# Plain fp32 products instead of split ones for the second block's gates and delta net

## The chip, the cores and the metric

One Trainium2 chip, one core. The metric is the device time of one execution, in microseconds (us), as the median of several. The engines are TensorE (PE; its weight loads are shown as PEld), VectorE (DVE), ScalarE (ACT), GpSimd (POOL), and SyncE (SP), which issues most DMAs. The granted TensorE clock is given as a share of full speed.

## The reference

Two blocks of a network on 256 tokens of width 1024, in fp32. The first (two layers of feed-forward, four attentions, feed-forward) isn't touched. The second mixes the tokens with two recurrent branches and then runs a mixture of experts. What matters here is the mixing sublayer, on the normed and modulated input `u_lat`:

```python
split_at = [A_COLS, A_COLS + B_COLS]
a_lat, b_lat, gates_lat = jnp.split(u_lat @ w_in, split_at, axis=-1)
oa_lat, _ = gdn_branch(a_lat, state_a, ...)              # gated delta net, 4 heads of 128
ob_lat, _ = rwkv_branch(to_col_major(b_lat, rows), state_b, ...)   # RWKV-7, 8 heads of 64
g_a, g_b = jnp.split(gates_lat, 2, axis=-1)
y = (sigmoid(g_a) * (o_a @ w_o_a) + sigmoid(g_b) * (o_b @ w_o_b)) @ w_out
```

`w_in` has 2064 columns for the delta net (q, k, v and z of 512 each, 16 for its decay and step), 1920 for the RWKV branch and 2048 for the gates.

## The kernel before, in words

Features lie on the 128 partitions, tokens along the free axis; a 1024-wide input is eight blocks `c` of [128, 256 tokens]. Most matrix products are **split products**: an fp32 operand is written as a high part, rounded by ScalarE (`split`: an activation Copy to fp32r), and a low part, the difference, taken by VectorE; `mm3` (lines 102 to 104) then adds three fp32r matmuls: low weights by high input, high by low, high by high. The weights are split as they arrive: a load `raw` of 1 MB holds 256 columns of all eight blocks, and each 128 columns of it take one ScalarE copy `wh` (L132) and one VectorE difference `wl` (L133), both [128, 1024]. Two raw buffers and three of split parts rotate.

The program is given as code; a scheduler with a model of the engines' times sets the order in which each engine gets its instructions, and each engine then works its queue in order. What is emitted under `high_priority(100000)` goes ahead of other work that is ready. The pools, which decide when a buffer comes free, act on that order too.

The second block's mixing sublayer is `mix` (L2182):

- `begin` norms the input (`norm_pair`, L175) and leaves it as a high part `hh` and a low part `hl`. It also stores both in a DRAM tensor `u_lat`, since SBUF is wanted for other things later. `hr` is the row factor that GpSimd's pow gives.
- `rwkv_proj` projects the RWKV columns (15 groups of 128; split products, evicted from the PSUM tile `pg`).
- `rwkv`, at high priority, treats the heads in two halves, called hf0 and hf1 here. For each: decay factors `first` (products `pw`), `second` (`pm` = A Bt for a chunk, from which DVE cuts `Ur`, `Mr`, `Mak`), the inverse of a unit triangular matrix (`inverse`, L951: diagonal blocks by row steps `Pb`, `Yb` on VectorE, then `ps_inv` matmuls L996 to L1044), the gate `pgate` (L1774, a plain fp32 product), the recurrence over four chunks (`pa` L1630, `psa` L1636, `pSr` L1648, `yr` L1619), and the output `ob`.
- `gdn_z` and `gdn_proj` project the delta net's columns with the same `proj` (L1059): z into `oa`, the 16 columns `ab`, then k, v, q, each through a short convolution `cvo` (L1093).
- `gates_ahead` projects the 2048 gate columns, 256 at a time. A weight load here is 128 KB (one block `c`, 256 columns); the weights are split by ScalarE (L2229) and GpSimd (L2230), and the two parts of the input come back from `u_lat` two blocks at a time (512 KB, two buffers). Tanh goes to a DRAM tensor `ths`.
- `gdn` prepares the delta net's factors, inverts its triangular matrix by the same routine (`U`), and runs its chain over chunks: `pks` (L1302), `pvn`, `pS`, `po`; `gdn_out` norms the result and multiplies it into `oa` (L1760).

Then `merge` (L2251) multiplies `oa` and `ob` by their output weights (split products `pb`), adds them under the gates (`merged`), and `out_proj` multiplies by `w_out` (`acc`). The router and the experts follow; their weights stream at some 350 GB/s with TensorE busy throughout, so this last part moves as a block with the merge's end.

Of the kernel before, what the change touches and what calls it, by code (L numbers as in the profile page):

```python
# [7 lines left out]
F32 = mybir.dt.float32  # L8
F32R = mybir.dt.float32r
I32 = mybir.dt.int32  # L10
AF = mybir.ActivationFunctionType
OP = mybir.AluOpType
# [3 lines left out]
P = 128  # L16
T = 256
D = 1024
KC = D // P
# [12 lines left out]
class Core:  # L32
# [139 lines left out]
        self.nc.vector.tensor_scalar(v, ss[:, 0:1], ss[:, 1:2], eps, op0=OP.add, op1=OP.add)  # L172
        return self.pow(pool, v, "%sr%d" % (name, t))

    def norm_pair(self, pool, x, rs, A, B=None, keep=None, save=None):  # L175

        nc = self.nc
        keep = keep or self.np  # L180
        hh = keep.tile([P, KC, T], F32R, tag="hh", name="hh")
        hl = keep.tile([P, KC, T], F32R, tag="hl", name="hl")
        for t in range(2):
            ts = slice(t * P, t * P + P)
            xn = [pool.tile([P, 512], F32, tag="xn", name="xn", bufs=4) for _ in range(2)]
            xs = [x[:, t, j * 512:j * 512 + 512] for j in range(2)]
            if B is not None:
                for j in range(2):
                    nc.vector.tensor_tensor(xn[j], xs[j], A[:, j], op=OP.mult)
            r = rs(t)  # L190
            for j in range(2):
                js = slice(4 * j, 4 * j + 4)
                if B is None:
                    nc.vector.scalar_tensor_tensor(xn[j], xs[j], r, A[:, j], op0=OP.mult, op1=OP.mult)
                else:
                    nc.vector.scalar_tensor_tensor(xn[j], xn[j], r, B[:, j], op0=OP.mult, op1=OP.add)
                pt = self.ps("s", [P, 4, P], "pt")
                for c in range(4):
                    nc.tensor.transpose(pt[:, c], xn[j][:, c * P:c * P + P], self.ident)
                last = self.split(hh[:, js, ts], hl[:, js, ts], pt)  # L200
            if save is not None:
                for i, v in enumerate((hh, hl)):
                    nc.sync.dma_start(out=save[:, i, :, ts], in_=v[:, :, ts].bitcast(F32))
            if t == 0:
                self.norm_ins0 = last
        self.norm_ins = last + (self.pow_ins,)
        return hh, hl
# [715 lines left out]
class Block2:  # L923
# [135 lines left out]
    def proj(self, u, w, start, n, evict):  # L1059

        k = self.k
        W = k.W
        wide = W.raw // KC
        cs = min(KC, W.part // P)
        for f0 in range(0, n, 256):
            pg = k.ps("g", [P, 2, T], "pg")
            for g0 in range(f0, min(f0 + 256, n), wide):
                m = min(wide, n - g0)
                wr = k.raw(w[:, start + g0: start + g0 + m].rearrange("(c p) f -> p c f", p=P), [P, KC, m])
                for h0 in range(0, m, P):  # L1070
                    mm = min(P, m - h0)
                    fi = (g0 + h0 - f0) // P
                    for c0 in range(0, KC, cs):
                        ws = k.split_w(wr[:, c0:c0 + cs, h0:h0 + mm])
                        for c in range(c0, c0 + cs):
                            k.mm3(pg[:mm, fi], (ws[0][:, c - c0], ws[1][:, c - c0]), (u[0][:, c], u[1][:, c]),
                                  c == 0, c == KC - 1)
            evict(f0 // P, (min(256, n - f0) + P - 1) // P, pg)
# [591 lines left out]
class Tail(Rwkv):  # L1670
# [476 lines left out]
    def begin(self, x, pool):  # L2147


        k, nc, a, R = self.k, self.k.nc, self.a, self.R  # L2150
        self.x1 = self.dram.tile([P, 2, D], F32, name="x1")
        self.u_lat = self.dram.tile([P, 2, KC, T], F32, name="u_lat")
        half = lambda v, q: v[:, q * 512:q * 512 + 512]
        with k.pool("lx", "right") as xp:
            fg, am, bm = [self.gk.tile([P, 2, 512], F32, name=n, tag=tag)
                          for n, tag in (("fg", "cv512"), ("am", "cv1024"), ("bm", "cv0"))]
            nc.sync.dma_start(out=fg.rearrange("p a b -> p (a b)"), in_=bcast_ap(a["final_norm"], D))
            self.row(0, am)
            self.row(1, bm)
            nc.vector.tensor_tensor(am, am, fg, op=OP.mult)  # L2160
            self.hr = self.cst.tile([P, 2], F32, name="hr")

            def both(t):

                xs, xf = [half(x[:, t], q) for q in range(2)], []
                for q in range(2):
                    xf.append(xp.tile([P, 512], F32, tag="mdg", name="xf", bufs=2))
                    nc.vector.tensor_tensor(xf[q], xs[q], fg[:, q], op=OP.mult)
                ss = k.sumsq(xp, xs, "hss")
                v = xp.tile([P, 1], F32, name="hv%d" % t)  # L2170
                nc.vector.tensor_scalar(v, ss[:, 0:1], ss[:, 1:2], 1e-6, op0=OP.add, op1=OP.add)
                ss = k.sumsq(xp, xf, "hsf")
                nc.vector.tensor_tensor(ss[:, 0:1], ss[:, 0:1], ss[:, 1:2], op=OP.add)
                nc.vector.scalar_tensor_tensor(ss[:, 0:1], v, 1e-6, ss[:, 0:1], op0=OP.mult, op1=OP.add)
                r = k.pow(xp, ss[:, 0:1], "hr%d" % t)
                nc.gpsimd.tensor_tensor(self.hr[:, t:t + 1], v, k.mhalf, op=OP.pow)
                return r
            nc.sync.dma_start(out=self.x1, in_=x)
            with k.use(s=k.banks["a"]):
                return k.norm_pair(xp, x, both, am, bm, pool, self.u_lat)  # L2180

    def mix(self, start):  # L2182


        k, a = self.k, self.a
        w = a["w_in_2"][0]
        with ExitStack() as right, ExitStack() as left:
            gk = self.gk = right.enter_context(k.pool("gk", "right"))
            gf = right.enter_context(k.pool("gf", "right"))
            proj = ExitStack()  # L2190
            up = proj.enter_context(k.pool("up", "right"))
            wp = Weights(proj.enter_context(k.pool("uw", "right")), 2048, 2, 1024, 3)
            u = start(up)
            lu = self.lat.enter_context(k.pool("lu"))
            oa = lu.tile([P, 4, T], F32, name="oa")
            ob = lu.tile([P, 4, T], F32, name="ob")
            k.regroup()
            G = dict(a=("a", 3), g=("a", 3), s=("a", 3), w=("w", 1))
            rk = left.enter_context(k.pool("rk"))
            rp = left.enter_context(k.pool("rp"))  # L2200
            with k.use(W=wp):
                self.keep, self.pool, self.t2 = rk, rp, 4
                cols = self.rwkv_proj(u, w, True)
                with k.tc.high_priority(100000):
                    self.rwkv(cols, self.Sb, True, "rl", None, ob)
                with k.use(**G), k.pool("gp", "right") as self.pool:
                    self.keep, self.t2 = gk, 2
                    self.gdn_z(u, w, oa)
                    gcols = self.gdn_proj(u, w, True)
            proj.close()  # L2210
            with k.pool("gm", "right") as self.pool, k.use(W=Weights(gf, 256, 4, 256, 2), **G):
                self.t2 = 4
                self.gates_ahead(gf, a["w_in_2"][0][:, 3984:6032])
                self.gdn_out(self.gdn(gcols, self.Sa, True, "gl"), oa)
        return oa, ob

    def gates_ahead(self, pool, w):

        k, nc = self.k, self.k.nc
        self.ths = self.dram.tile([P, 2 * KC, T], F32, name="ths")  # L2220
        for d in range(0, 2 * KC, 2):
            pg = k.ps("w", [P, 2, T], "pg")
            for c in range(KC):
                if c % 2 == 0:
                    u = pool.tile([P, 2, 2, T], F32, tag="u", name="u", bufs=2)
                    nc.sync.dma_start(out=u, in_=self.u_lat[:, :, c:c + 2])
                wr = k.raw(w[c * P:c * P + P, d * P:(d + 2) * P], [P, 256])
                ws = [k.W.parts.tile([P, 256], F32R, tag=tg, name=tg, bufs=k.W.npart) for tg in ("wh", "wl")]
                nc.scalar.activation(ws[0], wr, AF.Copy)  # L2229
                nc.gpsimd.tensor_tensor(ws[1], wr, ws[0].bitcast(F32), op=OP.subtract)  # L2230
                for j in range(2):
                    js = slice(j * P, j * P + P)
                    k.mm3(pg[:, j], (ws[0][:, js], ws[1][:, js]), (u[:, 0, c % 2].bitcast(F32R), u[:, 1, c % 2].bitcast(F32R)),
                          c == 0 and j == 0, c == KC - 1 and j == 1)
            th = self.pool.tile([P, 2, T], F32, tag="gth", name="gth")
            nc.scalar.activation(th, pg, AF.Tanh, scale=0.5)
            nc.sync.dma_start(out=self.ths[:, d:d + 2], in_=th)
# [193 lines left out]
```

## Time and profile before

| | |
|---|---|
| median of 3 runs | 2395.19 us (2394.86 to 2396.8) |
| profiled execution | 2390.7 us, of which the span 2389.0 |
| mean granted TensorE clock | 0.953 |
| PE busy | 2249.9 us (94%), 19065 records |
| DVE busy | 1689.7 us (71%) |
| ACT busy | 1199.8 us (50%) |
| POOL busy | 344.1 us (14%) |
| first block and the start of the second | 0 to 1616 us |
| second block's mixing sublayer | 1616 to 2032 us |
| out-projection, router, experts | 2032 to 2389 us |

How to read it: a share of the span is a mean over stages that have different limits, so the shares above say little on a change in one stage; the busy times by stage below do. Times in a timeline are from the span's start. A matmul's duration in the trace is longer than its share of the pipeline: one that follows another at once is best priced by the distance between the two starts. A plain fp32 matmul shows up as two records, a split product as three. A row's bracket gives the idle time of the engine before it and what ended it.

### The profile page before, as it was taken

To read this page: it belongs to the slowest core of one execution; us is meant where nothing else is said; L and a number is where in the kernel's file an instruction comes from. 1 tells how busy PE (TensorE), PEld (TensorE's weight loads), DVE (VectorE), ACT (ScalarE), POOL (GpSimd) and SP (SyncE) were. 2 spreads that over 40 slices of the span, in tenths; PEclk is the share of its full clock that TensorE was granted. 3 is DMA by queue.
4 is the path that set the end of the run, shared out by engine and by line. 5 is a ranking of instruction groups with operands and counts; after the bars stand their busy time and mean duration, and the time that the engine had idled before them with its cause. 6 is when DMAs were issued, how large, how long until landed. Compare 5 with 4: busy or idle time off the path is not lost. (4 is left out here: it accounts for less than half of the span.)

```text
span 2389.0 us, 46279 instructions
## 1 busy us (share of the span) xinstructions
PE 2249.9 (94%) x19065; PEld 2041.7 (85%) x19065; DVE 1689.7 (71%) x2796; ACT 1199.8 (50%) x1919; POOL 344.1 (14%) x465
## 2 busy tenths in 40 slices
PE   7999999999999999999999999998989887899997
PEld 6999988897889888888888979998877777799996
DVE  6775575766665674675856668886885866789997
ACT  5554455555443543544554554443553313477775
POOL 2000112121200100100122210002245511000000
PEclk9999999999999989999999999998988668899999
DMA  9676344455434334342545468986445415699992
GB/s 327 223 248 202 111 150 143 140 166 188 142 125 163 132 112 152 128 142 68 173 130 166 143 211 299 331 285 185 125 133 161 146 40 193 239 374 351 353 352 98
DMA packets 325166, 450.91 MB, mean 189 GB/s; under 512 B 16122, under 2 KB 253236, under 8 KB 324564
## 3 DMA queue, kind: packets, MB, share of 16 engines
q1 hardware_dynamic: 324276, 447.06, 55.9%
q8 instruction: 152, 2.49, 0.4%
q0 software_dynamic: 672, 0.82, 0.3%
q14 instruction: 66, 0.54, 0.1%
HBM read 438.09 MB, written 9.76 MB: 187 GB/s over the span
## 5 line engine op out<-in xcount | busy, mean ns | idle before, releaser
L133 DVE TENSOR_TENSOR wl<-raw,wh 128x1024 fp32r<-128x1024 f32 (+1 forms) x703 | 860.0, 1230 | 364.4 <-ACT wh L132 355.2
L132 ACT ACTIVATE wh<-raw 128x1024 fp32r<-128x1024 f32 (+1 forms) x703 | 730.5, 1043 | 465.8 <-PE pg L104 189.5
L102 PE MATMUL pg<-hh,wl 128*128 128x256 f32 x2176 | 627.9, 289 | 4.9 <-DVE wl L133 4.4
L103 PE MATMUL pg<-hl,wh 128*128 128x256 f32 x2176 | 625.9, 288 | 0.4 <-DVE hl L133 0.4
L104 PE MATMUL pg<-hh,wh 128*128 128x256 f32 x2176 | 625.8, 288 | 0.0
L102 PEld LDWEIGHTS pg<-hh,wl 128*128 128x128 f32 x2176 | 420.1, 193 | 17.2 <-issue 6.0
L103 PEld LDWEIGHTS pg<-hl,wh 128*128 128x128 f32 x2176 | 420.0, 193 | 11.1 <-issue 6.6
L104 PEld LDWEIGHTS pg<-hh,wh 128*128 128x128 f32 x2176 | 420.1, 193 | 7.8 <-issue 6.4
L102 PE MATMUL ph<-wh,m0t 128*128 128x256 f32 x512 | 146.4, 286 | 0.0
L102 PE MATMUL acc<-wh,ul 128*128 128x512 f32 x352 | 137.9, 401 | 8.7 <-DVE ul L133 7.0
L103 PE MATMUL ph<-wl,m0t 128*128 128x256 f32 x512 | 144.2, 282 | 0.1
L104 PE MATMUL ph<-wh,m0t 128*128 128x256 f32 x512 | 143.7, 281 | 0.0
L104 PE MATMUL acc<-wh,uh 128*128 128x512 f32 x352 | 140.7, 400 | 0.0
L103 PE MATMUL acc<-wl,uh 128*128 128x512 f32 x352 | 140.4, 399 | 0.0
L103 PE MATMUL acc<-wl,hh 128*128 128x512 f32 (+2 forms) x320 | 120.5, 377 | 0.0
L104 PE MATMUL acc<-wh,hh 128*128 128x512 f32 (+2 forms) x320 | 120.4, 378 | 0.0
L102 PE MATMUL acc<-wh,hl 128*128 128x512 f32 (+2 forms) x320 | 116.9, 381 | 0.5 <-DVE hl L133 0.5
L103 PEld LDWEIGHTS ph<-wl,m0t 128*128 128x128 f32 x512 | 96.5, 189 | 1.2 <-DVE wl L133 0.4
L104 PEld LDWEIGHTS ph<-wh,m0t 128*128 128x128 f32 x512 | 96.5, 188 | 0.5
L102 PEld LDWEIGHTS ph<-wh,m0t 128*128 128x128 f32 x512 | 96.7, 189 | 0.1
L454 ACT ACTIVATE sg<-pg 128x256 f32<-128x256 f32 x80 | 30.8, 385 | 127.4 <-PE pg L104 123.8
L1705 DVE SCALAR_TENSOR_TENSOR adacc<-raw,silu_c,adacc 128x512 f32<-128x512 f32 x112 | 83.4, 747 | 15.3 <-DMA raw<-in_ada_w_dram 14.7
(712 smaller groups left out, 4214.5 us busy)
## 6 DMA issues: line engine op xcount, KB each, us to landing
raw<-in_ffn_w_gu_dram SPq DMA_DIRECT2D x88, 1024.0 KB
raw<-in_w_in_dram SPq DMA_DIRECT2D x56, 1024.0 KB
raw<-in_ffn_w_down_dram SPq DMA_DIRECT2D x44, 1024.0 KB
raw<-in_w_gate_dram SPq DMA_DIRECT2D x32, 1024.0 KB
raw<-in_moe_w_gate_dram SPq DMA_DIRECT2D x32, 1024.0 KB
raw<-in_moe_w_up_dram SPq DMA_DIRECT2D x32, 1024.0 KB
raw<-in_moe_w_down_dram SPq DMA_DIRECT2D x32, 1024.0 KB
raw<-in_ada_w_dram SPq DMA_DIRECT2D x48, 512.0 KB
```

The source lines that it names most:

```text
L102: t.matmul(out, lhs[1], rhs[0], start=start, stop=False)
L103: t.matmul(out, lhs[0], rhs[1], start=False, stop=False)
L104: return t.matmul(out, lhs[0], rhs[0], start=False, stop=stop)
L132: return (nc.scalar.activation(h, src, AF.Copy), nc.vector.tensor_tensor(l, src, h.bitcast(F32), op=OP.subtract))
L133: nc.vector.tensor_tensor(l, src, h.bitcast(F32), op=OP.subtract))
L454: nc.scalar.activation(sg, pg[:, 0], AF.Silu)
L1705: nc.vector.scalar_tensor_tensor(acc, wv, sc, acc, op0=OP.mult, op1=OP.add)
```

## The change

For the second block's tokens, the delta net's projections and the gates use plain fp32 matmuls, with the weights as they are loaded and the input `uf` in full precision. `uf` [128, 8, 256] is a new SBUF tile, written by four GpSimd additions of `hh` and `hl` in `norm_pair`. The store of `u_lat` and its reloads are gone, and the gates' loads are 256 KB each (two blocks `c`), in four buffers. In `proj` the new path reads the raw buffer from TensorE itself. RWKV's projections, the merge and the experts keep split products.

```diff
@@ norm_pair
-            if save is not None:
-                for i, v in enumerate((hh, hl)):
-                    nc.sync.dma_start(out=save[:, i, :, ts], in_=v[:, :, ts].bitcast(F32))
+                if full is not None:
+                    nc.gpsimd.tensor_tensor(full[:, js, ts], hh[:, js, ts].bitcast(F32), hl[:, js, ts].bitcast(F32), op=OP.add)
@@ proj
+                    if not isinstance(u, (tuple, list)):
+                        for c in range(KC):
+                            k.nc.tensor.matmul(pg[:mm, fi], wr[:, c, h0:h0 + mm], u[:, c], start=c == 0, stop=c == KC - 1)
+                        continue
                     for c0 in range(0, KC, cs):
                         ws = k.split_w(wr[:, c0:c0 + cs, h0:h0 + mm])
@@ mix
+            self.uf = gf.tile([P, KC, T], F32, name="uf")
...
-                    self.gdn_z(u, w, oa)
-                    gcols = self.gdn_proj(u, w, True)
+                    self.gdn_z(self.uf, w, oa)
+                    gcols = self.gdn_proj(self.uf, w, True)
...
-            with k.pool("gm", "right") as self.pool, k.use(W=Weights(gf, 256, 4, 256, 2), **G):
+            with k.pool("gm", "right") as self.pool, k.use(W=Weights(gf, 512, 4, 0, 0), **G):
@@ gates_ahead
                 if c % 2 == 0:
-                    u = pool.tile([P, 2, 2, T], F32, tag="u", name="u", bufs=2)
-                    nc.sync.dma_start(out=u, in_=self.u_lat[:, :, c:c + 2])
-                wr = k.raw(w[c * P:c * P + P, d * P:(d + 2) * P], [P, 256])
-                ws = [k.W.parts.tile([P, 256], F32R, tag=tg, name=tg, bufs=k.W.npart) for tg in ("wh", "wl")]
-                nc.scalar.activation(ws[0], wr, AF.Copy)
-                nc.gpsimd.tensor_tensor(ws[1], wr, ws[0].bitcast(F32), op=OP.subtract)
+                    wr = k.raw(w[c * P:(c + 2) * P, d * P:(d + 2) * P].rearrange("(c p) f -> p c f", p=P), [P, 2, 256])
                 for j in range(2):
-                    js = slice(j * P, j * P + P)
-                    k.mm3(pg[:, j], (ws[0][:, js], ws[1][:, js]), (u[:, 0, c % 2].bitcast(F32R), u[:, 1, c % 2].bitcast(F32R)),
-                          c == 0 and j == 0, c == KC - 1 and j == 1)
+                    nc.tensor.matmul(pg[:, j], wr[:, c % 2, j * P:j * P + P], self.uf[:, c],
+                                     start=c == 0 and j == 0, stop=c == KC - 1 and j == 1)
```

The scheduler orders the changed program anew. Three places, with the line numbers of each program (those of the changed one are higher by 3 in this part, lower by 1 within the inverse):

TensorE's queue in hf0's recurrence, before: between `pa` and `psa` of the first chunk stand the transposes `ptk` for the delta net and four gate triples, of which one is shown.

```order
L1630 MATMUL pa<-Sb,AR 64x64 x8
L1105 MATMUL ptk<-ident,l2b 128x128
L1105 MATMUL ptk<-ident,cvo 128x128 x4
L102 MATMUL pg<-u,wl 128x256
L103 MATMUL pg<-u,wh 128x256
L104 MATMUL pg<-u,wh 128x256
...
L1105 MATMUL ptk<-ident,cvo 128x128 x4
L1636 MATMUL psa<-rhs,Ur 64x64 x8
```

The same place after (`pa` is L1633, `psa` L1639, the gate product L2230).

```order
L1622 MATMUL yr<-Sb,AR 64x64 x4
L2230 MATMUL pg<-uf,raw 128x256 x6
L1187 MATMUL rowp<-ident,Be 4x128
L1622 MATMUL yr<-Sb,AR 64x64 x4
L1633 MATMUL pa<-Sb,AR 64x64 x8
L2230 MATMUL pg<-uf,raw 128x256 x11
L1639 MATMUL psa<-rhs,Ur 64x64 x8
L2230 MATMUL pg<-uf,raw 128x256 x5
```

Eleven gate products stand where four triples stood, and the delta net's transposes come later in the queue; in this manner 86 of the 128 gate products lie in hf0's recurrence.

VectorE's queue at the row steps of the second half's inverse (`Pb_19364`, `Yb_19361`), before: they stand alone but for steps of other kinds; those of the delta net's inverse came earlier.

```order
L975 TENSOR_TENSOR Pb_19364<-Ub_19358,Yb_19361 128x49
L977 TENSOR_REDUCE Yb_19361<-Pb_19364 128x7
L975 TENSOR_TENSOR Pb_19364<-Ub_19358,Yb_19361 128x64
L977 TENSOR_REDUCE Yb_19361<-Pb_19364 128x8
L975 TENSOR_TENSOR Pb_19364<-Ub_19358,Yb_19361 128x81
L977 TENSOR_REDUCE Yb_19361<-Pb_19364 128x9
```

After: the steps of the delta net's inverse (`Pb_20715`, `Yb_20712`) and of the second half's alternate.

```order
L976 TENSOR_REDUCE Yb_20712<-Pb_20715 128x11
L974 TENSOR_TENSOR Pb_19364<-Ub_19358,Yb_19361 128x121
L974 TENSOR_TENSOR Pb_20715<-Ub_20709,Yb_20712 128x144
L976 TENSOR_REDUCE Yb_19361<-Pb_19364 128x11
L976 TENSOR_REDUCE Yb_20712<-Pb_20715 128x12
L974 TENSOR_TENSOR Pb_19364<-Ub_19358,Yb_19361 128x144
```

The two inverses that stood one behind the other now run side by side.

TensorE's queue where the delta net's chain begins, before: `pks` stands ahead of the second half's `pgate`, and its chain lies between the steps of that half's recurrence.

```order
L1302 MATMUL pks<-Sak,cvo 128x128 x4
L996 MATMUL ps_inv<-Yc,Q 32x32 x32
L1774 MATMUL pgate<-g_19680,lo 128x256 x2
L1778 MATMUL pv<-ident,vT 128x128 x4
L1619 MATMUL yr<-Sb,AR 64x64 x4
L1308 MATMUL pvn<-r,U 128x128 x4
L1619 MATMUL yr<-Sb,AR 64x64 x4
L1630 MATMUL pa<-Sb,AR 64x64 x8
L1314 MATMUL pS<-bv,kd 128x128 x4
```

After: the last steps of the delta net's inverse (L1036, L1043) lie in the last chunk of that recurrence, and `pks` (L1305) follows.

```order
L1633 MATMUL pa<-Sr,AR 64x64 x8
L1622 MATMUL yr<-Sr,AR 64x64 x8
L1036 MATMUL ps_inv<-D,U 64x64 x8
L1043 MATMUL ps_inv<-U,Q 64x64 x2
L1639 MATMUL psa<-rhs,Ur 64x64 x8
L1043 MATMUL ps_inv<-U,Q 64x64 x11
L1622 MATMUL yr<-SV,Mr 64x64 x8
L1043 MATMUL ps_inv<-U,Q 64x64 x3
L1305 MATMUL pks<-Sak,cvo 128x128 x4
L1311 MATMUL pvn<-r,U 128x128 x4
```

The chain of the delta net so stands behind the recurrence of the second half and not within it.

## Rows read from the trace of the kernel before

**Rows 1.** Busy us (records) by stage: PE, PEld, DVE, ACT, POOL; clock; DMA share; GB/s.

```profile
1633.00:1752.00 119.00, 115.58 (x932) 108.26 (x932) 90.54 (x159) 61.01 (x104) 34.19 (x38) 0.98 0.45 136
1752.00:1776.00 24.00, 16.95 (x120) 14.84 (x121) 22.86 (x63) 10.81 (x25) 8.73 (x13) 0.82 0.55 167
1776.00:1806.00 30.00, 23.32 (x607) 21.04 (x603) 13.44 (x30) 11.69 (x37) 15.31 (x20) 0.69 0.51 143
1806.00:1858.00 52.00, 49.18 (x576) 42.08 (x577) 32.34 (x75) 20.52 (x63) 29.49 (x33) 1.00 0.62 188
1858.00:1886.00 28.00, 20.80 (x121) 17.90 (x119) 23.55 (x53) 8.01 (x21) 13.35 (x19) 0.71 0.46 135
1886.00:1919.00 33.00, 30.95 (x304) 26.54 (x304) 27.55 (x54) 12.68 (x31) 17.11 (x22) 0.68 0.40 116
1919.00:1957.00 38.00, 28.05 (x1008) 26.21 (x998) 23.54 (x63) 5.92 (x12) 4.44 (x9) 0.53 0.16 49
1957.00:1995.00 38.00, 35.05 (x481) 30.68 (x476) 22.79 (x53) 8.31 (x28) 1.67 (x1) 0.90 0.30 101
```

**Rows 2.** Timeline, PE, full clock: start us, us, engine, line, tile, shape, records.

```profile
1214.54 0.59 PE L804 MATMUL sbs<-sbw,m_lt 128*128 128x256 f32 x2
1214.97 0.38 PE L805 MATMUL sbs<-sbw,ones 128*128 128x128 f32 x2
...
1808.07 0.28 PE L103 MATMUL pg<-u,wh 128*128 128x256 f32 x1
1808.19 0.29 PE L104 MATMUL pg<-u,wh 128*128 128x256 f32 x1
```

**Rows 3.** Timeline, PE, at the half clock.

```profile
1957.57 2.08 PE L1774 MATMUL pgate<-g,lo 128*128 128x256 f32 x4
...
1998.70 0.41 PE L102 MATMUL pb<-o,wl 128*128 128x256 f32 x1
1998.91 0.41 PE L103 MATMUL pb<-o,wh 128*128 128x256 f32 x1
```

**Rows 4.** Timeline, POOL, DVE and PE: the waits that the change touches; idle in brackets.

```profile
1628.33 1.40 POOL L2230 TENSOR_TENSOR wl<-raw,wh 128x256 fp32r<-128x256 f32 x2
...
1630.27 1.41 DVE L196 SCALAR_TENSOR_TENSOR xn<-xn,hr,bm 128x512 f32<-128x512 f32 x2 [2.07 <-POOL hr L165]
...
1646.30 0.36 PE L102 MATMUL pg<-u,wl 128*128 128x256 f32 x1 [1.99 <-DMA u<-u_lat]
```

**Rows 5.** Timeline: the first RWKV half's landmarks, PE.

```profile
1750.70 1.16 PE L1563 MATMUL pm<-AR,BK 64*128 64x128 f32 x16
...
1805.90 1.13 PE L1774 MATMUL pgate<-g,lo 128*128 128x256 f32 x4
...
1847.40 0.97 PE L1619 MATMUL yr<-SV,Mr 128*64 128x64 f32 x16
```

**Rows 6.** Costliest lines, 1500 to 2050: count, busy us, mean ns, idle and releasers.

```profile
L133 DVE TENSOR_TENSOR wl<-raw,wh 128x1024 fp32r<-128x1024 f32 (+1 forms) x85 | 106.9, 1262 | 33.0 <-ACT wh L132 32.9
...
L2230 POOL TENSOR_TENSOR wl<-raw,wh 128x256 fp32r<-128x256 f32 x64 | 50.0, 785 | 61.6 <-ACT wh L2229 59.3 <-issue 2.1
```

**Rows 7.** Tile pg alone by stage, columns as in rows 1: after 1806 only gates.

```profile
1806.00:1848.40 42.40, 17.00 (x114) 14.48 (x114) 0.00 (x0) 1.20 (x2) 1.00 0.61 184
1848.40:1886.00 37.60, 15.20 (x78) 12.37 (x78) 0.00 (x0) 1.19 (x2) 0.78 0.52 154
1886.00:1919.00 33.00, 16.08 (x72) 13.87 (x72) 0.00 (x0) 0.96 (x2) 0.68 0.40 116
```

**Rows 8.** Timeline: the end of the inverse, oa, and the merge.

```profile
1938.50 1.02 DVE L985 STREAM_TRANSPOSE Yc<-Ye 128x512 f32<-128x512 f32 x1
...
1994.34 0.75 DVE L1760 SCALAR_TENSOR_TENSOR oa<-pt,rowcols,oa 128x512 f32<-128x512 f32 x1 [0.72 <-PE pt L1758]
...
2013.65 0.55 PE L102 MATMUL pb<-o,wl 128*128 128x256 f32 x1 [3.82 <-DVE merged L251]
...
2031.98 1.08 PE L102 MATMUL acc<-wh,u 128*128 128x512 f32 x4
```

More of the change, by code (lines that the diff above doesn't have):

```diff
@@ L173, in rms, with norm_pair @@
         return self.pow(pool, v, "%sr%d" % (name, t))
-    def norm_pair(self, pool, x, rs, A, B=None, keep=None, save=None):
+    def norm_pair(self, pool, x, rs, A, B=None, keep=None, full=None):
         nc = self.nc
@@ L2151, in begin @@
         self.x1 = self.dram.tile([P, 2, D], F32, name="x1")
-        self.u_lat = self.dram.tile([P, 2, KC, T], F32, name="u_lat")
         half = lambda v, q: v[:, q * 512:q * 512 + 512]
@@ L2179, in begin @@
             with k.use(s=k.banks["a"]):
-                return k.norm_pair(xp, x, both, am, bm, pool, self.u_lat)
+                return k.norm_pair(xp, x, both, am, bm, pool, self.uf)
     def mix(self, start):
@@ L2207, in mix, with gates_ahead @@
                     self.keep, self.t2 = gk, 2
-                    self.gdn_z(u, w, oa)
-                    gcols = self.gdn_proj(u, w, True)
+                    self.gdn_z(self.uf, w, oa)
+                    gcols = self.gdn_proj(self.uf, w, True)
             proj.close()
-            with k.pool("gm", "right") as self.pool, k.use(W=Weights(gf, 256, 4, 256, 2), **G):
+            with k.pool("gm", "right") as self.pool, k.use(W=Weights(gf, 512, 4, 0, 0), **G):
                 self.t2 = 4
-                self.gates_ahead(gf, a["w_in_2"][0][:, 3984:6032])
+                self.gates_ahead(a["w_in_2"][0][:, 3984:6032])
                 self.gdn_out(self.gdn(gcols, self.Sa, True, "gl"), oa)
         return oa, ob
-    def gates_ahead(self, pool, w):
+    def gates_ahead(self, w):
         k, nc = self.k, self.k.nc
```

## The prediction

> **What bounds the kernel now.** I read the busy time by stage first, then the rows around each hand-over. The part that changes is the second block's mixing sublayer, 1633 to 1995 us; what follows it (merge, router, experts) is unchanged and moves with its end. In [rows 1] the reader is to see four kinds of stage. From 1633 to 1752 TensorE is busy 115.6 of 119 us at a granted clock of 0.98: the projections, bound by TensorE. From 1752 to 1806 and again from 1858 to 1957 TensorE has gaps and a clock of 0.53 to 0.82, while VectorE is busy 23.55 of 28, 27.55 of 33 and 23.54 of 38 us: here the small steps of the two triangular inverses and of second() set the pace. From 1806 to 1858 TensorE is busy 49.18 of 52 at full clock: the first RWKV half's recurrence, its pauses filled with gate products. From 1957 to 1995 it is busy 35.05 of 38 with the second half's recurrence and the delta net's chain lying into each other. So more TensorE work costs at once in the first and third kind of stage, and is partly free in the second, where before has put its gate triples; a step less on VectorE pays there.
>
> **The price of one product.** A split product is three records; they start 0.12 us apart, so it costs 0.36 us [rows 2]. Before has plain fp32 products of the same shape (128x128 by 128x256) in another stage: each is two records in the trace, and behind the one at 1214.54 the next line starts 0.43 us later [rows 2]. I take 0.43: +0.07 us each. At the half clock a split record takes 0.21 us, 0.64 for three, and a plain product between 0.85 (twice 0.43) and 1.04 (half of the 2.08 us at 1957.57) [rows 3]. The change has 136 such products in the delta net's projections (eight of them 16 columns wide) and 128 in the gates: 264 x 0.07 = 18.5 us more TensorE work at full clock.
>
> The Trainium skill, "FP8 and Floating Point Precision", section "TensorE Precision Notes", speaks against the change: a true fp32 product makes four passes through the array. If each pass cost the 0.12 us of a split record, the price would be 0.48, the addition 264 x 0.12 = 32 us, and hf0's recurrence below another 4 us longer; the row's 0.43, more than three passes and less than that, decides.
>
> **Ahead of and in the projections.** Two gate splits on GpSimd stand ahead of the norm's pow (1.40 us), and VectorE idles 2.07 us for that pow; one wait of 1.99 us for the reloaded input u stands in the triples [rows 4]. Both go: -3.3 us (1.3 + 2.0). The four gather-adds that write uf lie on GpSimd, which is free there; 38 unsplit triples (14 us) are ahead of uf's first reader. 136 x 0.07 = +9.5; nine gate products come in front of the last projection product (+3.9), four gate triples that before had there are gone (-1.4). The projections' end so comes 8.7 us later on TensorE. But that end isn't what hf0 waits for.
>
> **The first half (hf0), until its recurrence.** Its inverse waits for the last pm (1750.70 in before [rows 5]), and for VectorE, which stands in weight splits then. In after's order all triples come first, so pm's inputs are projected earlier, and the plain products stand behind: I lay the last pm at about 1745. Sixteen wide splits of 1.26 us [rows 6], 20 us of VectorE, are gone from the same stretch, so the inverse's steps find it free. Against it: 15 gate products now lie inside the inverse's matmuls (6.5 us at full clock, 13 at half), where before had gate triples too. Bounds for pgate: 14 us earlier (7 from pm, 7 from VectorE's queue) to 2 later (the projections' 8.7 delay all, less the 7 of VectorE). I take 8 earlier: 1798 instead of 1805.9 [rows 5].
>
> **hf0's recurrence.** In before it lasts from 1805.90 to 1848.37 [rows 5], with 114 gate records in it [rows 7], 38 triples or 13.7 us. After's order puts 86 plain gate products there, five to eleven at each pause, and moves the delta net's pk and pkq out: 86 x 0.43 = 37 us, and the other instructions of that stretch at the durations of the same lines are 17. TensorE was busy 49.18 of 52 us there with less, so nothing hides it: 54 us, last yr at 1852, 4 later than before. No gate product is left then, where before had 150 more records (78 and 72, [rows 7]), 50 triples or 18 us at full clock.
>
> **The tail until the second half's recurrence.** From 1858 to 1957 VectorE is busy 74.6 of 99 us [rows 1]. The two inverses, one mostly behind the other in before, now alternate on VectorE step by step, so each covers the other's waits. The rows of VectorE until both inverses are expanded sum to 73 us by their durations. GpSimd's 64 gate splits of 785 ns (50.0 us) [rows 6] are gone too; what their company costs VectorE no row here prices, so it goes into the lower bound. I take VectorE 90% busy: 73 / 0.9 = 81 us, so 1933 against 1938.5 + 1.0 [rows 8]; bounds 68 (no gap, and 7% off the durations for the company) and 91 (before's own pace, TensorE now at the half clock for want of gates). Before takes 19 us from there to pgate [rows 3, 8], so 1951: 7 us earlier.
>
> **The second half's recurrence and the delta net's chain.** Before runs them together: 1957.57 to oa's end at 1995.1, 37.5 us [rows 3, 8]. After's PE queue has pks of the delta net behind the second half's last psa and yr, since the delta net's inverse is now finished behind the other. The queue is in order, so the chain stands alone: the recurrence without gates 42.5 - 13.7 = 28 us, as in hf0, and then pks to oa, between 20 (half of the shared 37.5) and 38 (all of it); I take 30. 1951 + 58 = 2009, 14 later than before. Bounds of the pair: 48 and 75 (both at the half clock of the stage before).
>
> **Merge.** ob is ready before oa now, so its branch doesn't wait: before's second branch sat 3.82 us for merged [rows 8], and its last product stands ahead of 2031.98, 37 us after oa's end. In after 192 records follow oa without a pause, 0.12 each at full clock (23 us), 0.21 at half (41), with 1.4 us of split ahead; I take 28 + 1.4. End at 2039, 7 us after before's 2032.0 [rows 8].
>
> What costs nothing: the weights' buffers are held longer (16 products of 0.43, 6.9 us for 1 MB, two buffers), that is 152 GB/s, and [rows 1] shows 136 to 188 moved while nothing was short; the gate loads need 256 KB in 1.7 us, also 150. If this cover is gone, each megabyte costs about 2 us more, 17 of them.
>
> **Sum.** -8 (hf0's inverse), +12 (its recurrence: 54 for 42), -10 (from there to the second pgate: 99 for 109), +20 (the pair behind each other: 58 for 37.5), -7 (merge: 30 for 37) = +7 us. The profiled execution took 2390.7 us (span 2389.0), so 2398; the median of the runs shown is 4.5 us above it, so 2402.
>
> **Rivals.** (a) Faster: the relief of VectorE wins. Place: VectorE from 1745 to 1950; price: 20 us of splits, the gate splits' company, and the alternation, which hides the latency of two inverses; it decides once the tail takes less than 74 us, because pgate then stands before 1944 and the 48 us bound of the pair is near, as TensorE's work in it is only 35 us. 1942 + 49 + 29 = 2020, 12 us earlier: 2383. For it: the low busy shares of 1919 to 1957 in [rows 1], which are latency that alternation covers. Against it: hf0's recurrence is TensorE-bound and grows by 12. (b) No change: the pair takes 50 instead of 58, because the delta net's last inverse steps lie inside the recurrence and its pks comes at once: 2394. For it: before itself shows the two threads fit into 37.5 us. Against it: the order of the PE queue. (c) Much slower: without gate products the whole tail is at 0.5 clock, as 1919 to 1957 (0.53) was already in before; then the tail takes its bound of 91 us, pgate stands at 1961, the pair takes 62 (half way between its bounds) and the merge 33: 24 us later than before, 2419. (d) The weights' buffers starve the projections: 17 x 2 = 34 us, 2436.
>
> **Numbers.** Forecast (around 2402, its own range 2398 to 2410) 0.34; (a) 0.30; (b) 0.22; (c) 0.12; (d) 0.02. 0.2% (4.8 us) is about what a measurement of this kernel can tell from no change, so faster is below 2390.4: 0.30; same 0.22; slower 0.48. The range for 8 in 10 leaves out half of (a)'s far end, (d) and part of (c): 2381 to 2422.
>
> **What would show it.** Right: plain products 0.43 us apart; hf0's pgate before 1802; its recurrence 50 us or more with TensorE at 95%; the last gate before 1855; the TensorE clock of the stretch after it near 0.5; pks behind the last psa; pb without a break. Wrong: a plain product at 0.36 or less, or 0.48 and more; pks well before the recurrence's end, or the pair under 50 us (then a or b); gaps of TensorE in the projections that end on a raw load (then d).

## The result, and the profile after

The changed kernel took 2412.8 us (median of 5 runs, 2406.74 to 2416.11) against 2395.95 us (2394.86 to 2398.72) for the kernel before on the same chip: a ratio of 1.0066, 95% interval 1.0051 to 1.0081, 16.9 us slower. The profiled execution took 2409.9 us (span 2408.2), 19.2 us more than that of before. The forecast had 2402, slower, with a range from 2381 to 2422. Single executions of one kernel differ by several us: the profiled execution of before lies 5.3 us under the median here, that of the changed kernel 2.9, so stages are compared below to a few us and kernels by their medians.

Busy times by stage of the changed kernel, the windows of [rows 1] with one more for the merge; columns as there.

```profile
1633.00:1752.00 119.00, 118.78 (x794) 104.68 (x793) 74.96 (x149) 43.77 (x83) 32.63 (x43) 0.99 0.38 116
1752.00:1776.00 24.00, 16.71 (x84) 13.85 (x83) 21.74 (x65) 8.39 (x18) 0.31 (x1) 0.86 0.11 33
1776.00:1806.00 30.00, 26.68 (x627) 22.03 (x626) 7.14 (x14) 4.92 (x8) 2.34 (x4) 0.83 0.36 93
1806.00:1858.00 52.00, 51.65 (x481) 43.38 (x479) 12.02 (x31) 10.98 (x50) 5.88 (x5) 1.00 0.40 114
1858.00:1886.00 28.00, 22.73 (x104) 16.04 (x104) 20.08 (x53) 8.28 (x23) 15.28 (x14) 0.63 0.00 1
1886.00:1919.00 33.00, 25.25 (x169) 18.97 (x169) 29.76 (x63) 8.48 (x20) 14.27 (x18) 0.74 0.00 1
1919.00:1957.00 38.00, 11.88 (x655) 10.76 (x656) 24.33 (x85) 2.21 (x5) 2.32 (x4) 0.50 0.12 35
1957.00:1995.00 38.00, 30.97 (x830) 27.45 (x819) 20.39 (x44) 7.58 (x16) 4.81 (x9) 0.92 0.04 8
1995.00:2060.00 65.00, 54.33 (x365) 49.86 (x366) 46.77 (x63) 23.92 (x44) 9.44 (x5) 0.89 0.70 239
```

The reader is to see three things. From 1806 to 1858 TensorE is busy 51.65 of 52 us with VectorE down from 32.34 to 12.02: TensorE binds it and gate products fill it. From 1858 to 1995 GB/s is 1 to 35, so no gate weight is loaded any more, and from 1919 to 1957 TensorE works 11.88 us where it worked 28.05. And the delta net's chain runs on past 1995, where `oa` was done in before.

The timeline of TensorE in the changed kernel, at the places of [rows 2, 3, 5 and 8]:

```profile
1799.22 1.13 PE L1777 MATMUL pgate<-g,lo 128*128 128x256 f32 x4
...
1845.87 4.91 PE L2230 MATMUL pg<-uf,raw 128*128 128x256 f32 x22
1850.71 0.51 PE L1633 MATMUL pa<-Sr,AR 64*64 64x64 f32 x10
...
1856.83 0.46 PE L1622 MATMUL yr<-SV,Mr 128*64 128x64 f32 x8
...
1960.47 2.07 PE L1777 MATMUL pgate<-g,lo 128*128 128x256 f32 x4
...
1983.93 0.63 PE L1639 MATMUL psa<-rhs,Ur 64*64 64x64 f32 x13
...
1987.04 1.16 PE L1305 MATMUL pks<-Sak,cvo 128*128 128x128 f32 x8
...
2048.22 1.10 PE L102 MATMUL acc<-wh,u 128*128 128x512 f32 x4
```

Eleven gate products (22 records) start at 1845.87 and `pa` follows at 1850.71: 0.44 us for one. The last `psa` of the second half starts at 1983.93 and `pks`, the start of the delta net's chain, behind it, at 1987.04.

With the ends of the operations (`oa` ends at 2019.67) these landmarks cut the sublayer into stages; the same for each kernel that was run, all from one profiled execution each, in us (hf0's recurrence from the first `pgate` to the end of the last `yr`; the last column counts records in the trace, of which some are missing):

| kernel | first pgate at | hf0's recurrence | tail, to second pgate | pair, to oa's end | merge, to first acc | from there to the end | span | gate products behind hf0's recurrence |
|---|---|---|---|---|---|---|---|---|
| before | 1805.9 | 42.5 | 109.2 | 37.5 | 36.9 | 357.0 | 2389.0 | 50 triples |
| changed | 1799.2 | 58.1 | 103.2 | 59.2 | 28.5 | 360.0 | 2408.2 | 0 |
| e1 delta net first | 1796.7 | 58.4 | 97.3 | 40.6 | 28.6 | 362.0 | 2383.6 | 32 |
| e2 before, delta net first | 1813.7 | 44.2 | 97.6 | 41.8 | 35.7 | 359.6 | 2392.6 | 63 triples |
| e3 gates only | 1799.7 | 54.9 | 101.5 | 43.4 | 28.6 | 359.9 | 2388.0 | 0 |
| e4 half the gates | 1801.3 | 39.0 | 105.2 | 54.5 | 27.5 | 359.8 | 2387.3 | 0 |
| e5 e1, chain late | 1801.1 | 58.2 | 97.1 | 53.3 | 27.2 | 358.4 | 2395.2 | 32 |
| e6 e1, 64 held | 1805.1 | 42.1 | 109.1 | 36.2 | 37.5 | 358.2 | 2388.1 | 63 |
| e7 e1, 96 held | 1803.5 | 35.8 | 114.1 | 34.6 | 37.6 | 359.2 | 2384.9 | 88 |
| e8 changed, 64 held | 1799.0 | 35.9 | 112.1 | 63.8 | 27.9 | 359.8 | 2398.5 | 53 |
| e9 e7, gates only | 1798.7 | 40.8 | 107.1 | 45.2 | 32.7 | 362.7 | 2387.1 | 94 |
| e10 e1, 112 held | 1793.8 | 44.0 | 119.0 | 43.9 | 26.9 | 361.0 | 2388.6 | 104 |

From before to the changed kernel: -6.7 (first pgate), +15.6 (recurrence), -6.0 (tail), +21.7 (pair), -8.4 (merge), +3.0 (rest) = +19.2 us.

Not all of this is the change's. The second block's first instruction on VectorE starts 1.8 us earlier in the changed kernel, before anything that was changed; before's line first:

```profile
1616.57 1.28 DVE L189 TENSOR_TENSOR xn<-x,am 128x512 f32<-128x512 f32 x2
```

```profile
1614.79 1.28 DVE L189 TENSOR_TENSOR xn<-x,am 128x512 f32<-128x512 f32 x2
```

Over the twelve kernels it starts between 1614.0 (e1) and 1620.9 (e7), although the first block is the same in all. From this line on, the first `pgate` comes 4.9 us earlier than in before (184.4 for 189.3), not 6.7.

### The profile page after: what moved, and what is told of

The parts are those of the page before. It is cut to its first block, busy times and chain, and to the rows that moved or that the text cites. A ratio compares the mean times of both kernels' runs of the same rounds, so it can differ in the third digit from the quotient of the medians.

```text
span 2408.2 us, 45333 instructions
## 1 busy us (share of the span) xinstructions
PE 2254.1 (94%) x18801; PEld 2025.8 (84%) x18801; DVE 1654.9 (69%) x2779; ACT 1159.7 (48%) x1838; POOL 299.1 (12%) x405
## 5 line engine op out<-in xcount | busy, mean ns | idle before, releaser
L133 DVE TENSOR_TENSOR wl<-raw,wh 128x1024 fp32r<-128x1024 f32 (+1 forms) x686 | 839.8, 1232 | 354.0 <-ACT wh L132 344.0
L132 ACT ACTIVATE wh<-raw 128x1024 fp32r<-128x1024 f32 (+1 forms) x686 | 713.1, 1044 | 452.6 <-PE pg L104 176.9
L102 PE MATMUL pg<-hh,wl 128*128 128x256 f32 x2040 | 587.3, 288 | 3.6 <-DVE wl L133 3.1
L103 PE MATMUL pg<-hl,wh 128*128 128x256 f32 x2040 | 585.5, 287 | 1.6 <-DVE hl L133 1.6
L104 PE MATMUL pg<-hh,wh 128*128 128x256 f32 x2040 | 585.6, 287 | 0.0
L102 PEld LDWEIGHTS pg<-hh,wl 128*128 128x128 f32 x2040 | 393.4, 193 | 14.5 <-issue 5.0
L103 PEld LDWEIGHTS pg<-hl,wh 128*128 128x128 f32 x2040 | 393.3, 193 | 11.4 <-issue 5.9
L104 PEld LDWEIGHTS pg<-hh,wh 128*128 128x128 f32 x2040 | 393.5, 193 | 7.2 <-issue 6.1
L1708 DVE SCALAR_TENSOR_TENSOR adacc<-raw,silu_c,adacc 128x512 f32<-128x512 f32 x112 | 83.7, 749 | 15.7 <-DMA raw<-in_ada_w_dram 14.9
```

The source lines that it names most:

```text
L102: t.matmul(out, lhs[1], rhs[0], start=start, stop=False)
L103: t.matmul(out, lhs[0], rhs[1], start=False, stop=False)
L104: return t.matmul(out, lhs[0], rhs[0], start=False, stop=stop)
L132: return (nc.scalar.activation(h, src, AF.Copy), nc.vector.tensor_tensor(l, src, h.bitcast(F32), op=OP.subtract))
L133: nc.vector.tensor_tensor(l, src, h.bitcast(F32), op=OP.subtract))
L1708: nc.vector.scalar_tensor_tensor(acc, wv, sc, acc, op0=OP.mult, op1=OP.add)
```

## The experiments

Three theories were on record. A: the order does it; gate products, now ready at once, fill the first half's recurrence and push the delta net's preparation back, and its chain then stands alone. B: the price; 264 products cost more on TensorE. C: the clock; without gate products the tail runs at the half clock.

### e1 and e2: the delta net ahead of the gates

The scheduler takes what was emitted first among the work that is ready. e1 is the changed kernel with two lines swapped, e2 the kernel before with the same swap.

```diff
-                self.gates_ahead(a["w_in_2"][0][:, 3984:6032])
                 self.gdn_out(self.gdn(gcols, self.Sa, True, "gl"), oa)
+                self.gates_ahead(a["w_in_2"][0][:, 3984:6032])
```

> The changed kernel with the delta net's scan emitted ahead of the gates, so that a ready gate product no longer goes before the delta net's preparation. Theory A (order: gate products delay the delta net's factors, and its chain then stands alone behind the second half's recurrence): the pair from the second pgate to oa falls from 59 to 38 to 44 us, the first half's recurrence stays within 5 us of its 58, the end comes 12 to 20 us earlier, 2393 to 2401. Theory B (price: 264 products at 0.44 instead of 0.36 are simply more TensorE work): the same work in another order, 2408 to 2414. Theory C (clock: without gate products the stretch from 1858 to 1960 runs at half clock): this order leaves some 40 gate products behind the first half's recurrence, so the clock there rises and a third of the loss comes back, 2405 to 2408.

Measured: 2390.64 us against 2397.79 for before on that chip, ratio 0.9970 (0.9955 to 0.9985). The changed kernel was 0.7% slower than before and is now 0.3% faster with the same work in another order: the order is worth 1% of the time, and A's mechanism holds. It is worth more than A had, as the median lies 2 us under A's range. The pair falls to 40.6 us, as A said; the recurrence stays at 58.4, with 60 gate products in it where the changed kernel has 86, since products for the delta net's factors came in (422 other records for 370). TensorE of e1 from the second `pgate`, and `oa` on VectorE:

```profile
1952.43 2.08 PE L1777 MATMUL pgate<-g,lo 128*128 128x256 f32 x4
...
1957.21 1.16 PE L1305 MATMUL pks<-Sak,cvo 128*128 128x128 f32 x8
1958.61 0.77 PE L1639 MATMUL psa<-rhs,Ur 64*64 64x64 f32 x16 [0.24 <-DVE rhs L1635]
...
1984.08 0.68 PE L1639 MATMUL psa<-rhs,Ur 64*64 64x64 f32 x16
...
1991.59 1.41 DVE L1763 SCALAR_TENSOR_TENSOR oa<-pt,rowcols,oa 128x512 f32<-128x512 f32 x2 [0.19 <-PE pt L1761]
```

`pks` now stands ahead of the first `psa` and not behind the last.

> The kernel before with the delta net's scan emitted ahead of the gates. It tells whether this order is worth the same without the change. Theory A: before already has the delta net's factors in the first half's recurrence and its chain within the second half's, so there is little to win: 2391 to 2399. If the order alone is worth what e1 gains, this run is 12 us or more faster than before, and e1 says nothing on the change. Theories B and C: no difference from before, within 3 us.

Measured: 2395.28 us, ratio 0.9984 (0.9968 to 0.9999). So the swap is worth 0.16% to before and some 1% to the changed kernel: it undoes something that the change brought. B and C had no difference within 3 us; it was 2.5, so this run alone doesn't speak against them.

On C: the clock of e1 and of the changed kernel, first in the tail's second part (windows from 1886 to the second `pgate`), then in the whole tail; e1's two lines first:

```profile
1886.00:1952.00 66.00, 52.99 (x1226) 45.87 (x1227) 45.23 (x105) 14.05 (x31) 13.03 (x19) 0.50 0.08 24
1855.13:1952.43 97.30, 76.75 (x1375) 66.55 (x1374) 74.09 (x178) 21.18 (x52) 23.01 (x31) 0.63 0.13 38
```

```profile
1886.00:1960.00 74.00, 38.97 (x876) 31.32 (x878) 54.09 (x147) 11.10 (x25) 16.59 (x22) 0.61 0.07 21
1857.29:1960.47 103.18, 62.53 (x992) 47.89 (x992) 74.79 (x200) 20.06 (x51) 31.87 (x36) 0.62 0.05 15
```

In the second part e1's clock is lower (0.50 against 0.61), in the whole tail the two are the same (0.63 and 0.62). C had the loss come back through a higher clock of the tail; all of it came back without one, so C falls as the cause of the loss.

### e3: only the gates plain

```diff
-                    self.gdn_z(self.uf, w, oa)
-                    gcols = self.gdn_proj(self.uf, w, True)
+                    self.gdn_z(u, w, oa)
+                    gcols = self.gdn_proj(u, w, True)
```

> Only the gates with plain products; the delta net's projections stay split. In this order the delta net's chain lies within the second half's recurrence again, while gate products fill the first half's as in the changed kernel. Theory A: the first half's recurrence 52 us or more, the pair about 40, the whole 2398 to 2404. Theory B: 128 of 264 products, about half of the 17 us: 2403 to 2406. Theory C: no gate product is left for the tail, so all of the loss stays: 2410 to 2414.

Measured: 2398.24 us, ratio 0.9991 (0.9974 to 1.0008): no change from before, and so 0.75% under the whole change. A is nearest, and B (2403 to 2406) and C (2410 to 2414) are out: the recurrence is filled nearly as in the changed kernel (54.9 us), the pair is 43.4. That part of the change makes no measurable loss alone, although it fills the recurrence; the chain lies within the second half's recurrence here (`pks` 7.2 us after the second `pgate`), and by A that is the reason. The converse, only the delta net plain, has no run.

### e4: half of the gates' work left out

Four of eight blocks of the gates' contraction are left out, with their loads.

```diff
-            for c in range(KC):
+            for c in range(KC // 2):
```

> The changed kernel with only the first half of the gates' contraction (four of eight blocks, 64 of 128 products; the other half of the input is left out). Theories A and B: each product left out of the first half's recurrence is worth 0.44 us there; some 40 of them are gone from it, so it takes 58 - 18 = 40 us; with the delta net's factors earlier the pair takes 50 or less: 2380 to 2392. Theory C: the tail has no gate products either way, so only the recurrence's 18 us come back: 2394 to 2397.

Measured: 2389.63 us, ratio 0.9957 (0.9941 to 0.9973). The recurrence takes 39.0 us (40 expected), though not by the sum expected: by the trace 54 products fewer lie in it, not 40, for 19.1 us, 0.35 each, since TensorE now pauses for 3.2 us in it and a few transposes for the delta net came in. But the pair stays at 54.5 (50 or less expected), as `pks` comes late in this order too (1965.8, 20 us behind the second `pgate`). With half of the gate products gone this kernel is 0.43% faster than before, some 10 us, and the pair is still 17 us longer than in before.

### e5: the chain held back, nothing else

e1 with one edge on TensorE's queue: `pks` behind the second half's last `psa` (which the recurrence notes in `ends`; not shown).

```diff
-                    for h in range(4):
+                    with k.behind(*getattr(self, "ends", [])[1:2]):
+                      for h in range(4):
                         nc.tensor.matmul(pk[:, h], kTd[d][:, h, n * P:n * P + P], S[:, h, d], start=True, stop=True)
```

> The kernel of e1 (delta net emitted ahead of the gates), with one edge more: the delta net's pks wait in TensorE's queue for the second half's last psa, as in the changed kernel. All else stays as in e1. Theory A (the chain behind the recurrence costs 20 us): e1's pair of 40.6 us becomes 55 to 60, less 5 to 8 that the merge gives back, so 9 to 14 us slower than e1: 2400 to 2405. Theory B (only the amount of TensorE work counts): as e1, 2390 within 3. Theory C (half clock for want of gate products): as e1 within 3.

Measured: 2399.65 us, ratio 1.0009 (0.9994 to 1.0024), 0.39% above e1's, some 9 us, as A had it; B and C had no difference. TensorE and VectorE of e5 at the same places:

```profile
1956.31 2.08 PE L1779 MATMUL pgate<-g,lo 128*128 128x256 f32 x4
...
1977.58 0.68 PE L1640 MATMUL psa<-rhs,Ur 64*64 64x64 f32 x16 [0.22 <-DVE rhs L1636]
1978.19 1.16 PE L1306 MATMUL pks<-Sak,cvo 128*128 128x128 f32 x8
...
2008.20 1.41 DVE L1765 SCALAR_TENSOR_TENSOR oa<-pt,rowcols,oa 128x512 f32<-128x512 f32 x2 [1.00 <-PE pt L1763]
```

The pair grows from 40.6 to 53.3 us by this one edge: 12.7, less than the 15 to 20 that A had. The recurrence without company takes 21.3 us to its last `psa`, the chain 31.4 from `pks` to `oa`'s end. So the chain's place is shown to be a cause, with a price of 12.7 of the 21.7 us; e1's order keeps some 3 more than before (40.6 against 37.5), and the other 6 are what the changed kernel has over e5: its last `psa` comes 23.5 us after `pgate` (2.2 more), `pks` 3.1 later (2.5 more), and from there it is 32.6 to the end (1.2 more). The last steps of the delta net's inverse, which the changed kernel has inside that recurrence, may make the first two; that was not tried.

### e6, e7, e10 and e8: gate products held behind the first half's recurrence

The products of the later groups get an edge behind the first half's last `psa`; e6 holds four of eight groups (`d >= 8`, shown), e7 six (`d >= 4`), e10 seven (`d >= 2`), all on e1; e8 holds four on the changed kernel itself.

```diff
-                    nc.tensor.matmul(pg[:, j], wr[:, c % 2, j * P:j * P + P], self.uf[:, c],
+                    with k.behind(*(self.ends[:1] if d >= 8 else ())):
+                        nc.tensor.matmul(pg[:, j], wr[:, c % 2, j * P:j * P + P], self.uf[:, c],
```

> The changed kernel with its own emission order, and the last four groups of gate products held behind the first half's last psa. The delta net's chain still stands behind the second half's recurrence. Theory A: the recurrence falls from 58 to 38 to 42 us, but the gates go ahead of the delta net's factors in the tail, which grows by 5 to 15 us; the pair stays at 57 to 62: 2398 to 2408. Theory B: as the changed kernel, 2408 to 2414. Theory C: the higher clock of the tail wins most of it back, 2392 to 2398.

Measured: 2402.92 us, ratio 1.0017 (1.0001 to 1.0032), 0.5% under the changed kernel. The recurrence falls by 22.2 us, more than expected, for 53 products that leave it, 0.42 each; the tail grows by 8.9, 0.17 each. That is the other half of A, shown apart from the first: the pair stays long (63.8). It is even 4.6 longer than in the changed kernel, as `pks` comes 32.6 us after the second `pgate` and 11 after the last `psa`; that fits gate products in the tail that put off the delta net's inverse, and wasn't tried apart. With this, a product moved out of the recurrence costs 0.25 elsewhere, against the 0.42 that it cost there.

> The kernel of e1, with the last four of eight groups of gate products (64 of 128) held behind the first half's last psa, so that they lie in the tail. Theory A (products in the first half's recurrence cost 0.44 us each, in the tail they are partly free): the recurrence falls from 58 to 46 to 50 us, the tail to the second pgate grows by 2 to 8: 2384 to 2391. Theory B: as e1, 2388 to 2393. Theory C: the tail gets more products and a higher clock, 5 us or more faster than e1: below 2386.

Measured: 2389.23 us, ratio 0.9964 (0.9949 to 0.9978). The same as e1 within the intervals: the recurrence gives 16.3 us, more than expected, and the tail takes 11.8 of it, more than expected as well, both for 31 products by the trace (0.38 each in the tail); the merge goes back to 37.5 us, its `pb` again in before's order (48 records, transposes for `ob`, 144).

> As e6, but six of eight groups (96 products) held behind the first half's last psa. Theory A: the recurrence falls to 35 to 40 us, the tail has 42 us of plain products at full clock beside its own work and grows by 10 to 18: 2385 to 2395. Theory B: as e1. Theory C: the clock of the tail rises to 0.8 and more, and the end comes before e6's.

Measured: 2386.13 us, ratio 0.9947 (0.9928 to 0.9966): the lowest median of all, 12 us under before on that chip, though its interval overlaps those of e1, e6 and e10. The recurrence is down to 35.8 us, the tail up by 16.8 against e1. Its windows, from the recurrence on:

```profile
1803.00:1839.00 36.00, 30.53 (x406) 22.07 (x403) 21.43 (x48) 8.07 (x34) 12.10 (x10) 0.95 0.03 9
1839.00:1886.00 47.00, 44.30 (x254) 35.52 (x252) 36.90 (x92) 10.33 (x27) 14.50 (x16) 0.93 0.30 85
1886.00:1953.00 67.00, 59.57 (x1287) 49.21 (x1287) 46.00 (x109) 14.74 (x32) 12.22 (x19) 0.75 0.15 43
1953.00:1988.00 35.00, 31.95 (x484) 28.60 (x480) 22.59 (x53) 8.76 (x28) 1.67 (x1) 1.00 0.40 136
```

The clock of the tail's second part is 0.75 instead of e1's 0.50 (0.82 in the whole tail), as C wanted, and the tail, with 56 products more in it, is longer, not shorter. C's other sign, an end before e6's, holds by 3 us in the medians and not beyond the intervals.

> As e7, but seven of eight groups (112 products) held behind the first half's last psa. Theory A: past e7's point the tail and the second half's recurrence take the products at 0.44 us and more: 2385 to 2394, not faster than e7. Theory C: a tail at a still higher clock, faster than e7 by 3 us or more. Theory B: as e7.

Measured: 2387.76 us, ratio 0.9954 (0.9935 to 0.9973), not to be told from e7. The tail takes 119.0 us, and two products reach into the second half's recurrence: holding more gives nothing, as A said. One stage shows what the clock can cost. hf0's recurrence has the same 391 records on TensorE in e7 and e10; e7's line is first:

```profile
1803.50:1839.32 35.82, 30.35 (x391) 21.89 (x390) 20.96 (x48) 8.15 (x35) 12.10 (x10) 0.96 0.03 9
```

```profile
1793.78:1837.82 44.04, 39.05 (x391) 27.31 (x390) 21.11 (x48) 8.35 (x35) 12.06 (x10) 0.73 0.04 9
```

It takes 8.2 us longer at a clock of 0.73 than at 0.96, and TensorE's busy time grows by 8.7. In the 30 us ahead of it TensorE was busy 17.6 us in e10 and 22.1 in e7.

### e9: e7 with the delta net's projections split

The edit of e3 on e7.

> The kernel of e7 with the delta net's projections split again (triples), so that only the gates are plain. Theory A: 136 products cost 0.08 us less each on TensorE, 11 us in a stretch that TensorE binds, but 16 wide splits return to VectorE and the first pgate comes where it stood in before, 1806; the two nearly cancel: 2383 to 2392. Theory B (price alone): 11 us faster than e7, 2375 to 2378. Theory C: as e7.

Measured: 2389.58 us, ratio 0.9968 (0.9956 to 0.9981), 0.2% above e7 with intervals that overlap. B is out: by price alone 136 products split again should have given 11 us. A's total holds, but not its step: the first `pgate` came at 1798.7 and not at 1806; the pair is longer instead (45.2 for 34.6, with 54 records of gate products between its steps).

## Why the prediction was right or wrong

The sign, the range and the two mechanisms that the forecast rested on (gate products that fill hf0's recurrence, and a chain that stands behind the second half's) were right; the size was not: +7 us forecast, +19.2 in the profile and +16.9 in the medians. The median of 2412.8 lies inside the wide range and above the forecast's own, 2398 to 2410. Each step:

- **Price of a product.** 0.43 taken, 0.44 measured. This step was right, and e1, with the same products and faster than before, shows that the price as such doesn't make the loss. The Trainium skill's page "FP8 and Floating Point Precision", section "TensorE Precision Notes", states four passes for a true fp32 product. The trace fits this, since 0.44 is 3.7 times the 0.12 of a split record, but it shows two records for a product and no passes.
- **The first pgate.** 1798 forecast, 1799.2 measured: right in part by luck. 1.8 us of the 6.7 stand at the second block's start already, so the mixing itself gave 4.9 of the 8 forecast, and by a path that the forecast didn't have whole. VectorE had the inverse's diagonal ready at 1774.2, and the first `ps_inv` starts at 1778.65, because eleven gate products stand ahead of it in the queue and these had waited 7.29 us for PSUM:

```profile
1764.06 0.42 PE L1168 MATMUL pab<-ident,ab 16*128 16x16 f32 x4
1770.16 1.06 ACT L1099 ACTIVATE cvo<-cvo 128x1024 f32<-128x1024 f32 x1 [7.42 <-DVE cvo L1096]
1771.13 0.58 ACT L2233 ACTIVATE gth<-pg 128x512 f32<-128x512 f32 x1
1771.76 6.96 PE L2230 MATMUL pg<-uf,raw 128*128 128x256 f32 x22 [7.29 <-ACT gth L2233]
1778.65 1.26 PE L995 MATMUL ps_inv<-Yc,Ur 32*32 32x16 f32 x128
```

  The first group's tanh stood on ScalarE behind the convolution's Silu, which waited 7.42 us for VectorE; the gates have one PSUM buffer in the program. From 1774.2 to 1778.65 is 4.5 us on the path to the first pgate. It was read from the trace and not tried apart.
- **hf0's recurrence.** +12 forecast (54 us), +15.6 measured (58.1). The mechanism is shown by e8; the term was mis-sized by 4: the other instructions of that stretch, 17 us by my sum of durations, take 58.1 - 86 x 0.44 = 20.
- **The tail.** -10 forecast, -6.0 measured. VectorE was to take 81 us, 90% busy, and `pgate` to follow 18 us later (the 19 in the text is 18 by its own rows, 1939.5 to 1957.57). It took 83.7 (1857.3 to 1941.0, 87% of it for the 73 us of rows), and `pgate` 19.5. In this last part VectorE waits for TensorE's small inverse products nearly all the time:

```profile
1943.42 0.88 DVE L1002 TENSOR_SCALAR Q<-ps_inv,halves 128x256 f32<-128x256 f32 x2 [2.46 <-PE ps_inv L995]
1949.34 0.42 DVE L1005 TENSOR_TENSOR Yc<-Yc,ps_inv 128x256 f32<-128x256 f32 x1 [5.04 <-PE ps_inv L995]
1953.10 0.42 DVE L1006 TENSOR_TENSOR Yc<-Yc,ps_inv 128x256 f32<-128x256 f32 x1 [3.34 <-PE ps_inv L995]
```

  The row steps alternated on VectorE nearly without gaps towards the end, as rival (a) had it (busy 35.7 of the 36 us from 1905 to 1941), but preparation of the delta net, which before had in the first recurrence, lies in the same tail; with part of it ahead (e1) the tail takes 97.3. This last part, from VectorE's last transpose for the inverses to `pgate`, takes 18.1 us in before, 19.5 in the changed kernel and 17.3 in e1, all at a clock of 0.50, and 21.1 in e7 at 0.83 with gate products in it.
- **The pair.** +20 forecast (58), +21.7 measured (59.2): right in sum. Its parts were off against each other: the recurrence alone takes 23.5 to its last `psa` and not 28 (42.5 - 13.7 is 28.8), the chain 32.6 and not 30, and 3 us lie between.
- **The merge.** -7 forecast, -8.4 measured: right; `ob` was ready, and the 192 records ran on after one wait of 0.63 us behind the first.
- **Behind the merge** the forecast had nothing, and 3.0 us came: 360.0 for 357.0 us from the first `acc` to the end. All kernels that were run have 358.2 to 362.7 there, e2 with split products too. The stage also has the router, which doesn't stream weights at 350 GB/s (2060 to 2080 of before: 121 GB/s). What makes the 3.0 isn't settled; one execution each can't tell it from chance, since the first block, which is the same in all, ends up to 6.9 apart.

So no one term explains the miss of 12.2 us: five errors (3.1 for the first pgate, 3.6, 4, 1.7, 3) point one way, and the merge's 1.4 and the second block's start with 1.8 the other. The largest two are hf0's recurrence and the tail, with the causes read from the trace above. Of the rivals, (a) came true in its place and not in its price; (b) didn't happen, as the pair took 59; (d), starved projections, neither, TensorE being busy 118.78 of 119 us there. (c) came nearer in time than the forecast did, +24 for +19.2 and +16.9, but not by its mechanism: the tail took 103.2 us at a clock of 0.62 and not 109 at 0.5, and e1 won the loss back at the same clock. Its second `pgate` at 1961 (measured 1960.5) is a chance hit, made of a longer recurrence and a shorter tail.

## What to carry to other kernels

When a producer that paced filler work is taken away (here 50 us of GpSimd splits), a scheduler can place the filler at once, where it is ready, and not where it is free: look where it lands, what it delays, and what is then left to fill the stages that have room. Emission order was worth more here than the whole change: two swapped lines took it from 0.7% slower to 0.3% faster. Holding back 96 products besides gave 0.5%, which these runs can't tell from 0.3%. Small errors of a sum that nearly all lie on the optimistic side add up, and a landmark that agrees with the forecast can owe it to a stage before the change; a stretch that is bound by one engine should be summed with every instruction in it at the distance of starts, not by durations from a stretch where others hid it.

## What was not expected of the hardware

- What the clock cost depended on the stage. The tail took 97.3 us in e1 and 103.2 in the changed kernel at the same granted clock (0.63 and 0.62), and 114.1 in e7 at 0.82 with 56 more products in it: there the amount and the order of the work decide. hf0's recurrence, with the same records in e7 and e10, took 35.8 us at 0.96 and 44.0 at 0.73: there the clock was paid for.
- A plain fp32 product that moved into the tail cost it 0.17 us (e8, 53 products; 0.25 with the longer pair), 0.30 (e7 against e1, 56) or 0.38 (e6 against e1, 31). One that left hf0's recurrence gave 0.42 (e8), 0.43 (e7, 52 products) or 0.52 (e6), and 0.35 in e4, where TensorE's pauses stayed open.
